# A prefix-sum diagonal kernel: small PSUM copies moved from ScalarE to VectorE, and the last tiles cut up differently

## The chip, the cores and the metric

The kernel runs on one core of a Trainium2 chip. The metric is the device time of one execution in microseconds (us). Executions of one kernel agree within about 0.3%, and all runs told of here are of the fast state with the full granted TensorE clock (1.0). Engines are named as in the profile: PE (matrix multiply), DVE (VectorE), ACT (ScalarE), POOL (GpSimd), SP (the engine that issues the input DMAs).

## The reference

```python
def reference(x):                      # x: (4, 4224, 4224) float32
    ps = np.cumsum(np.cumsum(x, axis=1), axis=2)
    diag = np.diagonal(ps, axis1=1, axis2=2)
    return np.cumsum(diag, axis=1).astype(np.float32)   # (4, 4224)
```

All of x, 285 MB, has to be read once. The output is 68 KB.

## The kernel before

Each batch is cut into 33 tiles of 128 rows and all 4224 columns (2112 KB). For tile I the kernel makes three things: ACT sums each row up to the end of the diagonal block (`rp_full`); DVE multiplies the diagonal block with a triangular mask (`du`, with its row sums in `rp_du`) and adds the tile into a running column sum `acc`; PE sums `du` and a block of `acc` over the rows into `cp_ps`. From these comes one number per row, `s = rp_full - rp_du + cp_ps`. Two prefix passes on PE then turn the numbers of one batch into its output. Each pass needs small results copied from PSUM to SBUF between its matmuls:

```python
def cumsum_pass1(x_sb):
    nc.tensor.matmul(cs_ps, lhsT=u_incl, rhs=x_sb, start=True, stop=False)
    nc.tensor.matmul(a_ps, lhsT=x_sb, rhs=ones_col, start=True, stop=True)
    nc.scalar.copy(a_sb, a_ps)                     # ACT
    nc.tensor.matmul(p_ps, lhsT=a_sb, rhs=u_strict[0:NB, 0:NB], ...)
    nc.scalar.copy(p_sb, p_ps)                     # ACT
    nc.tensor.matmul(cs_ps, lhsT=ones_row, rhs=p_sb, start=False, stop=True)
    nc.vector.tensor_copy(t_sb, cs_ps)             # DVE
# pass 2: again two ACT copies (a2_sb, p2_sb); its result stays in PSUM (ot_ps)
```

In the last batch the passes run early, over tiles 0 to 30, and the last two tiles are added by short extra matmuls. The last tile (32) comes in ten pieces, 1408, 896, 640, 384, 256 and five times 128 columns, so that its sums can start before all of it is there:

```python
for ci, (c0, c1) in enumerate(last_chunks):        # ten pieces
    nc.scalar.activation(out=act_scratch[:, c0:c1], in_=xt[:, c0:c1],
                         func=Copy, accum_out=rp_parts[:, ci : ci + 1])
    # ... pre += rp_parts of this piece (DVE), but for the last piece
# ... after the loop, in this order:
pre2 = pre - rp_du[:, LAST]; pre2 += cp_ps[:, LAST]        # DVE
delta = pre2 + rp_parts[:, NPART - 1]                      # DVE
nc.tensor.matmul(ot_ps[LAST], lhsT=delta, rhs=ramp_ut, start=False, stop=True, ...)
nc.scalar.copy(ot_sb[LAST], ot_ps[LAST])
nc.scalar.dma_start(out=out_by_block[b, LAST], in_=ot_sb[LAST])   # rows 0 to 31 went out before
```

Of the kernel before, what the change touches and what calls it, by code (L numbers as in the profile page):

```python
# [9 lines left out]
FP32 = mybir.dt.float32  # L10
# [4 lines left out]
def kernel(  # L15
# [5 lines left out]
    nc = tc.nc  # L21

    B, H, W = x.shape
# [8 lines left out]
    fast_tail = (LAST % 32 == 0) and NB >= 4 and B >= 1  # L32
# [43 lines left out]
    def make_last_chunks():  # L76
        sizes = []
        remaining = W
        first = True
        while remaining > 0:  # L80
            if first:
                size = min(remaining, max(P, (remaining // (3 * P)) * P))
                first = False
            else:
                size = max(P, min((2 * sizes[-1] + P) // (3 * P) * P, remaining))
            size = min(size, remaining)
            sizes.append(size)
            remaining -= size
        chunks = [(W - sizes[0], W)]
        start = 0  # L90
        for s in sizes[1:]:
            chunks.append((start, start + s))
            start += s
        assert start == W - sizes[0]
        return chunks

    last_chunks = make_last_chunks() if fast_tail else [(0, W)]
    NPART = len(last_chunks)

    def cumsum_pass1(x_sb):  # L100
# [4 lines left out]
        a_sb = smalls.tile([NB, 1], FP32, name="a_sb")  # L105
        nc.scalar.copy(a_sb, a_ps)  # L106
# [4 lines left out]
        p_sb = smalls.tile([1, NB], FP32, name="p_sb")  # L111
        nc.scalar.copy(p_sb, p_ps)  # L112
        nc.tensor.matmul(cs_ps, lhsT=ones_row, rhs=p_sb, start=False, stop=True)  # L113
        t_sb = smalls.tile([P, NB], FP32, name="t_sb")
        nc.vector.tensor_copy(t_sb, cs_ps)  # L115
        return t_sb

    def cumsum_pass2_transposed(t_sb, ot_ps):
# [3 lines left out]
        a2_sb = smalls.tile([NB, 1], FP32, name="a2_sb")  # L122
        nc.scalar.copy(a2_sb, a2_ps)  # L123
# [4 lines left out]
        p2_sb = smalls.tile([1, NB], FP32, name="p2_sb")  # L128
        nc.scalar.copy(p2_sb, p2_ps)  # L129
# [4 lines left out]
    for b in range(B):  # L134
# [4 lines left out]
        rp_parts = perbatch.tile([P, NPART + 1], FP32, name="rp_parts")  # L139
# [7 lines left out]
        if last_batch:  # L147
            s31mat = smalls.tile([P, 32], FP32, name="s31mat")
            nc.vector.memset(s31mat, 0.0)
            pre = smalls.tile([P, 1], FP32, name="pre")  # L150
            delta = smalls.tile([P, 1], FP32, name="delta")
            s31 = smalls.tile([P, 1], FP32, name="s31")

        for I in range(NB):
# [16 lines left out]

            chunked = last_batch and I == LAST and NPART > 1
            xt = tiles.tile([P, W], FP32, name="xt")
            if not chunked:
# [8 lines left out]
            if not chunked:  # L183
                nc.scalar.activation(  # L184
                    out=act_scratch[:, 0 : P * (I + 1)],
                    in_=xt[:, 0 : P * (I + 1)],
                    func=mybir.ActivationFunctionType.Copy,
                    accum_out=rp_full[:, I : I + 1],
                )
            else:  # L190
                for ci, (c0, c1) in enumerate(last_chunks):
# [13 lines left out]
                    elif 1 < ci < NPART - 1:  # L205
# [5 lines left out]
                        )  # L211

# [43 lines left out]
        if not last_batch:  # L256
# [8 lines left out]
            nc.scalar.copy(ot_sb, ot_ps)  # L265
# [3 lines left out]
        nc.vector.tensor_tensor(  # L269
            out=s31,  # L270
            in0=rp_full[:, LAST - 1 : LAST],
            in1=rp_du[:, LAST - 1 : LAST],
            op=mybir.AluOpType.subtract,
        )
        nc.vector.tensor_tensor(
            out=s31,
            in0=s31,
            in1=cp_ps[:, LAST - 1 : LAST],
            op=mybir.AluOpType.add,
        )  # L280
        nc.vector.tensor_copy(out=s31mat[:, 31:32], in_=s31)
        nc.tensor.matmul(
            ot_ps[0:32, :],
            lhsT=s31mat,
            rhs=ramp_ut,
            start=False,
            stop=True,
            skip_group_check=True,
        )
        nc.tensor.matmul(  # L290
            ot_ps[LAST : LAST + 1, :],
            lhsT=s31,
            rhs=ramp_full,
            start=False,
            stop=False,
            skip_group_check=True,
        )
        nc.scalar.copy(ot_sb[0:LAST, :], ot_ps[0:LAST, :])
        nc.gpsimd.dma_start(out=out_by_block[b, 0:LAST, :], in_=ot_sb[0:LAST, :])

        if NPART == 1:
            base_ap = rp_full[:, LAST : LAST + 1]
        elif NPART == 2:
            base_ap = rp_parts[:, 0:1]
        else:
            base_ap = pre
        pre2 = smalls.tile([P, 1], FP32, name="pre2")
        nc.vector.tensor_tensor(
            out=pre2,
            in0=base_ap,  # L310
            in1=rp_du[:, LAST : LAST + 1],
            op=mybir.AluOpType.subtract,
        )
        nc.vector.tensor_tensor(
            out=pre2,
            in0=pre2,
            in1=cp_ps[:, LAST : LAST + 1],
            op=mybir.AluOpType.add,
        )
        if NPART > 1:  # L320
            nc.vector.tensor_tensor(
                out=delta,
                in0=pre2,
                in1=rp_parts[:, NPART - 1 : NPART],
                op=mybir.AluOpType.add,
            )
        else:
            delta = pre2
# [43 lines left out]
```

## Time and profile before

| | before |
|---|---|
| time, median of 13 runs | 686.09 us |
| span of the program in the profile | 684.0 us |
| last byte of x landed (semaphore updates in the trace) | 673.64 us |
| from there to the end of the span | 10.4 us |

From the page of the kernel before: busy time of the engines with their share of the span, then the busy share of DVE, ACT and the DMA engines in 40 slices, in tenths (9 is 90% or more), and the rate of the DMAs.

```profile
PE 146.1 (21%) x590; PEld 129.3 (19%) x590; DVE 326.4 (48%) x424; ACT 284.7 (42%) x304; POOL 4.0 (1%) x16
...
DVE  3876553321587654322078756432118775542211
ACT  1122344566312334556711234456661222454675
...
DMA  9999999999999999999999999999999999999991
GB/s 369 431 429 428 428 428 428 429 429 429 428 426 430 428 429 429 428 428 427 429 428 429 430 428 427 430 428 429 429 428 427 429 430 427 430 428 428 428 421 66
```

The DMA row is at 9 in every slice but the last. The rate is level at about 428 GB/s and no other engine is full. So in all but the last of the 40 slices the kernel moves at the speed of its input. The chain of waits (the chain of work that ended last, followed back; shares by engine and by line) says the same:

```profile
DMA 85%; DVE 6%; ACT 6%; issue 1%; PE 1%; SPq 0%; DVEq 0%; ACTq 0%
DMA xt<-in_x_dram 85%; ACT act_scratch L184 5%; DVE acc L249 5%; ACT act_scratch L192 1%; DVE du L214 0%; DVE acc L245 0%; PE cs_ps L113 0%; PE cs_ps L102 0%; SPq L175 0%; PE ot_ps L119 0%; PE ot_ps L329 0%; PE p_ps L108 0%; PE a_ps L104 0%; DVE t_sb L115 0%; ACT p_sb L112 0%
```

What is left for a change is the end. This is ACT's timeline there: start in us, duration in us, engine, source line, operation, out<-in with shapes, and in brackets how long ACT was idle before it and what ended the wait. (Each sum is followed by a 0.19 us step that reads its accumulator; those rows are left out, and the shorter pieces too.)

```profile
663.18 3.51 ACT L184 ACTIVATE act_scratch<-xt 128x3968 bf16<-128x3968 f32 x1 [1.54 <-DMA xt<-in_x_dram]
...
668.23 0.15 ACT L106 COPY a_sb<-a_ps 33x1 f32<-33x1 f32 x1 [1.45 <-PE a_ps L104]
668.74 0.18 ACT L112 COPY p_sb<-p_ps 1x33 f32<-1x33 f32 x1 [0.35 <-PE p_ps L108]
670.62 0.15 ACT L123 COPY a_sb<-a_ps 33x1 f32<-33x1 f32 x1 [1.71 <-PE a_ps L121]
671.13 0.18 ACT L129 COPY p_sb<-p_ps 1x33 f32<-1x33 f32 x1 [0.35 <-PE p_ps L125]
671.21 3.61 ACT L184 ACTIVATE act_scratch<-xt 128x4096 bf16<-128x4096 f32 x1
...
674.82 1.36 ACT L192 ACTIVATE act_scratch<-xt 128x1408 bf16<-128x1408 f32 x1
...
679.90 0.29 ACT L192 ACTIVATE act_scratch<-xt 128x128 bf16<-128x128 f32 x1
...
681.60 0.26 ACT L337 COPY ot_sb<-ot_ps 1x128 f32<-1x128 f32 x1 [1.17 <-PE ot_ps L329]
681.89 0.50 ACTq L338 DMA_DIRECT2D out_dram<-ot_sb  x1
```

Tile 31 had landed at 668.23, in the middle of this, but its sum (4096 columns, L184) starts at 671.21. Ahead of it in ACT's order stand four copies that each wait for PE. From then on ACT is never idle: tile 31, then ten pieces one after the other, until 680.28, the last accumulator read included. All pieces had landed by 673.64, so nothing here waits for data any more.

DVE's timeline at the very end shows what follows the last pieces: the additions into `pre`, two more for `rp_du` and `cp_ps`, and `delta` (L321), which PE waits for.

```profile
678.86 1.32 DVE L206 TENSOR_TENSOR pre<-pre,rp_parts 128x1 f32<-128x1 f32 x5 [0.24 <-ACT act_scratch L192]
680.22 0.16 DVE L308 TENSOR_TENSOR pre<-pre,rp_du 128x1 f32<-128x1 f32 x1
680.42 0.16 DVE L314 TENSOR_TENSOR pre<-pre,cp_ps 128x1 f32<-128x1 f32 x1
680.68 0.16 DVE L321 TENSOR_TENSOR delta<-pre,rp_parts 128x1 f32<-128x1 f32 x1
```

### The profile page before, as it was taken

To read this page: it belongs to the slowest core of one execution; us is meant where nothing else is said; L and a number is where in the kernel's file an instruction comes from. 1 tells how busy PE (TensorE), PEld (TensorE's weight loads), DVE (VectorE), ACT (ScalarE), POOL (GpSimd) and SP (SyncE) were. 2 spreads that over 40 slices of the span, in tenths; PEclk is the share of its full clock that TensorE was granted. 3 is DMA by queue.
4 is the path that set the end of the run, shared out by engine and by line. 5 is a ranking of instruction groups with operands and counts; after the bars stand their busy time and mean duration, and the time that the engine had idled before them with its cause. 6 is when DMAs were issued, how large, how long until landed. Compare 5 with 4: busy or idle time off the path is not lost.

```text
span 684.0 us, 2514 instructions
## 1 busy us (share of the span) xinstructions
PE 146.1 (21%) x590; PEld 129.3 (19%) x590; DVE 326.4 (48%) x424; ACT 284.7 (42%) x304; POOL 4.0 (1%) x16
## 2 busy tenths in 40 slices
PE   0121121221411212212132112121122221221213
PEld 0121121111311211112122112121122111111212
DVE  3876553321587654322078756432118775542211
ACT  1122344566312334556711234456661222454675
POOL 1000000000000000000000000000000000000000
DMA  9999999999999999999999999999999999999991
GB/s 369 431 429 428 428 428 428 429 429 429 428 426 430 428 429 429 428 428 427 429 428 429 430 428 427 430 428 429 429 428 427 429 430 427 430 428 428 428 421 66
DMA packets 20447, 285.69 MB, mean 418 GB/s; under 512 B 2336, under 2 KB 3282, under 8 KB 3666
## 3 DMA queue, kind: packets, MB, share of 16 engines
q1 hardware_dynamic: 20304, 285.48, 98.2%
q8 instruction: 4, 0.07, 0.0%
q0 software_dynamic: 128, 0.07, 0.0%
q14 instruction: 9, 0.07, 0.0%
q10 hardware_dynamic: 2, 0.00, 0.0%
HBM read 285.47 MB, written 0.07 MB: 417 GB/s over the span
## 4 chain that ended last, share of the span: by engine, by line
DMA 85%; DVE 6%; ACT 6%; issue 1%; PE 1%; SPq 0%; DVEq 0%; ACTq 0%
DMA xt<-in_x_dram 85%; ACT act_scratch L184 5%; DVE acc L249 5%; ACT act_scratch L192 1%; DVE du L214 0%; DVE acc L245 0%; PE cs_ps L113 0%; PE cs_ps L102 0%; SPq L175 0%; PE ot_ps L119 0%; PE ot_ps L329 0%; PE p_ps L108 0%; PE a_ps L104 0%; DVE t_sb L115 0%; ACT p_sb L112 0%
## 5 line engine op out<-in xcount | busy, mean ns | idle before, releaser
L184 ACT ACTIVATE act_scratch<-xt 128x128 bf16<-128x128 f32 (+10 forms) x131 | 262.5, 2004 | 378.4 <-DMA xt<-in_x_dram 378.4
L249 DVE TENSOR_TENSOR acc<-acc,xt 128x3968 f32<-128x3968 f32 (+30 forms) x124 | 283.6, 2287 | 0.0
L214 DVE CUSTOM_DVE_ANT_0 du<-xt,u_strict 128x128 f32<-128x128 f32 x132 | 38.5, 292 | 322.0 <-DMA xt<-in_x_dram 322.0
L224 PE MATMUL cp_ps<-ones_col,du 128*128 128x1 f32 x264 | 77.3, 362 | 512.0 <-DVE rp_du L214 512.0
L224 PEld LDWEIGHTS cp_ps<-ones_col,du 128*128 128x128 f32 x264 | 66.1, 311 | 524.3 <-DVE rp_du L214 513.7
L234 PE MATMUL cp_ps<-ones_col,acc 128*128 128x1 f32 x256 | 72.4, 352 | 0.0
L234 PEld LDWEIGHTS cp_ps<-ones_col,acc 128*128 128x128 f32 x256 | 70.0, 333 | 0.0
L184 ACT ACTIVATION_READ_ACCUMULATOR act_scratch<-xt 128x1 f32 x131 | 24.4, 186 | 0.0
L214 DVE DVE_READ_ACCUMULATOR2_ANT rp_du<- 128x1 f32 x132 | 10.9, 82 | 0.3
L245 DVE COPY acc<-xt 128x4096 f32<-128x4096 f32 x4 | 9.2, 2290 | 0.0
L257 DVE TENSOR_TENSOR s_sb<-rp_full,rp_du 128x33 f32<-128x33 f32 x3 | 0.6, 196 | 10.5 <-ACT act_scratch L184 10.5
L192 ACT ACTIVATE act_scratch<-xt 128x128 bf16<-128x128 f32 (+5 forms) x10 | 5.4, 537 | 0.0
L115 DVE COPY t_sb<-cs_ps 128x33 f32<-128x33 f32 x4 | 0.8, 194 | 9.0 <-PE cs_ps L113 9.0
L102 PE MATMUL cs_ps<-s_sb,u_incl 128*128 128x33 f32 x8 | 2.6, 413 | 11.7 <-DVE s_sb L260 8.9
L266 POOL DMA_DIRECT2D out_dram<-ot_sb x3 | 1.7, 575 | 511.8 <-ACT ot_sb L265 511.8
L102 PEld LDWEIGHTS cs_ps<-s_sb,u_incl 128*128 128x128 f32 x8 | 2.0, 312 | 12.0 <-DVE s_sb L260 9.2
L123 ACT COPY a_sb<-a_ps 33x1 f32<-33x1 f32 x4 | 0.6, 153 | 6.8 <-PE a_ps L121 6.8
L106 ACT COPY a_sb<-a_ps 33x1 f32<-33x1 f32 x4 | 0.6, 153 | 5.8 <-PE a_ps L104 5.8
L119 PE MATMUL ot_ps<-u_incl,t_sb 128*33 128x128 f32 x8 | 2.5, 422 | 1.1 <-DVE t_sb L115 1.1
L113 PE MATMUL cs_ps<-p_sb,u_incl 1*128 1x33 f32 x8 | 2.5, 408 | 1.1 <-ACT p_sb L112 1.1
L130 PE MATMUL ot_ps<-u_incl,p_sb 1*33 1x128 f32 x8 | 2.5, 416 | 1.1 <-ACT p_sb L129 1.1
L113 PEld LDWEIGHTS cs_ps<-p_sb,u_incl 1*128 1x128 f32 x8 | 2.0, 308 | 1.8 <-ACT p_sb L112 1.8
(50 smaller groups left out, 23.0 us busy)
## 6 DMA issues: line engine op xcount, KB each, us to landing
xt<-in_x_dram SPq DMA_DIRECT2D x131, 2112.0 KB, 27.2
xt<-in_x_dram SPq DMA_DIRECT2D x1, 704.0 KB, 23.8
xt<-in_x_dram SPq DMA_DIRECT2D x1, 448.0 KB, 24.4
xt<-in_x_dram SPq DMA_DIRECT2D x1, 320.0 KB
xt<-in_x_dram SPq DMA_DIRECT2D x5, 64.0 KB, 5.0
xt<-in_x_dram SPq DMA_DIRECT2D x1, 192.0 KB, 24.3
xt<-in_x_dram SPq DMA_DIRECT2D x1, 128.0 KB, 19.6
out_dram<-ot_sb POOLq DMA_DIRECT2D x3, 16.5 KB, 5.6
```

The lines of the kernel that those rows point to most:

```text
L102: nc.tensor.matmul(cs_ps, lhsT=u_incl, rhs=x_sb, start=True, stop=False)
L113: nc.tensor.matmul(cs_ps, lhsT=ones_row, rhs=p_sb, start=False, stop=True)
L119: nc.tensor.matmul(ot_ps, lhsT=t_sb, rhs=u_incl, start=True, stop=False)
L130: nc.tensor.matmul(ot_ps, lhsT=p2_sb, rhs=ones_row, start=False, stop=True)
L184: nc.scalar.activation(out=act_scratch[:, 0 : P * (I + 1)], in_=xt[:, 0 : P * (I + 1)], func=mybir.ActivationFunctionType.Copy, accum_out= ...
L192: nc.scalar.activation(out=act_scratch[:, c0:c1], in_=xt[:, c0:c1], func=mybir.ActivationFunctionType.Copy, accum_out=rp_parts[:, ci : ci ...
L214: nc.vector.tensor_tensor_reduce(out=du, in0=xt[:, P * I : P * (I + 1)], in1=u_strict, scale=1.0, scalar=0.0, op0=mybir.AluOpType.mult, op ...
L224: nc.tensor.matmul(cp_ps[:, I : I + 1], lhsT=du, rhs=ones_col, start=False, stop=False, skip_group_check=True,)
L234: nc.tensor.matmul(cp_ps[:, I : I + 1], lhsT=acc[:, P * I : P * (I + 1)], rhs=ones_col, start=False, stop=False, skip_group_check=True,)
L245: nc.vector.tensor_copy(out=acc[:, P * (I + 1) :], in_=xt[:, P * (I + 1) :])
L249: nc.vector.tensor_tensor(out=acc[:, P * (I + 1) :], in0=acc[:, P * (I + 1) :], in1=xt[:, P * (I + 1) :], op=mybir.AluOpType.add,)
L266: nc.gpsimd.dma_start(out=out_by_block[b], in_=ot_sb)
```

## The change

Its intent is to shorten this tail: take the copies out of ACT's order, fetch and sum tile 31 in halves, cut tile 32 into four pieces, give part of tile 30 to DVE, and send the output of the last batch in one DMA. Cut to its core:

```diff
+    last_chunks: four pieces, (2816,4224) (0,1280) (1280,2304) (2304,2816), not ten
+
+    def psum_to_sbuf(name, src):
+        dst = smalls.tile(list(src.shape), FP32, name=name)
+        nc.vector.tensor_copy(dst, src)
+        return dst
...
-        nc.scalar.copy(a_sb, a_ps)
+        a_sb = psum_to_sbuf("a_sb", a_ps)          # p_sb, a2_sb, p2_sb likewise, in all batches
...
+            split31 = last_batch and I == LAST - 1 and NPART > 1
+            if split31:
+                for (c0, c1) in ((0, W // 2), (W // 2, W)):
+                    nc.sync.dma_start(out=xt[:, c0:c1], in_=x[b, P*I : P*(I+1), c0:c1])
...
+            elif split31:        # two ACT sums, 0:2112 and 2112:4096, and a DVE addition
...
+            elif last_batch and I == LAST - 2 and NPART > 1:
+                half = P * (I + 1) - 1408          # ACT sums 0:2560, DVE the other 1408 columns
+                nc.vector.reduce_sum(out=rp_parts[:, NPART + 3 : NPART + 4],
+                                     in_=xt[:, half : P * (I + 1)], axis=X)
...
-            nc.scalar.copy(ot_sb, ot_ps)           # batches 0 to 2
+            nc.vector.tensor_copy(ot_sb, ot_ps)
...
-        nc.scalar.copy(ot_sb[0:LAST, :], ot_ps[0:LAST, :])
-        nc.gpsimd.dma_start(out=out_by_block[b, 0:LAST, :], in_=ot_sb[0:LAST, :])
+        with tc.high_priority():                   # around the whole tail
...
+            nc.scalar.copy(ot_sb, ot_ps)
+            nc.scalar.dma_start(out=out_by_block[b], in_=ot_sb)     # all 33 rows at once
```

More of the change, by code (lines that the diff above doesn't have):

```diff
@@ L30 @@
     N_TILE_BUFS = 6
-    fast_tail = (LAST % 32 == 0) and NB >= 4 and B >= 1
+    fast_tail = (LAST % 32 == 0) and NB >= 4
     consts = ctx.enter_context(tc.tile_pool(name="consts", bufs=1))
@@ L74 @@
     ones_row = u_incl[0:1, :]
-    def make_last_chunks():
-        sizes = []
-        remaining = W
-        first = True
-        while remaining > 0:
-            if first:
-                size = min(remaining, max(P, (remaining // (3 * P)) * P))
-                first = False
-            else:
-                size = max(P, min((2 * sizes[-1] + P) // (3 * P) * P, remaining))
-            size = min(size, remaining)
-            sizes.append(size)
-            remaining -= size
-        chunks = [(W - sizes[0], W)]
-        start = 0
-        for s in sizes[1:]:
-            chunks.append((start, start + s))
-            start += s
-        assert start == W - sizes[0]
-        return chunks
-    last_chunks = make_last_chunks() if fast_tail else [(0, W)]
+    if fast_tail and W >= 8 * P:
+        c_a = (W // 3) // P * P
+        c_d = min(4 * P, max(P, (W // 8) // P * P))
+        rem = W - c_a - c_d
+        c_b = max(P, (rem * 3 // 5) // P * P)
+        c_c = rem - c_b
+        sizes = [c_a, c_b, c_c, c_d]
+        assert all(s >= P for s in sizes) and sum(sizes) == W
+        last_chunks = [
+            (W - c_a, W),
+            (0, c_b),
+            (c_b, c_b + c_c),
+            (c_b + c_c, c_b + c_c + c_d),
+        ]
+    else:
+        last_chunks = [(0, W)]
     NPART = len(last_chunks)
+    def psum_to_sbuf(name, src):
+        dst = smalls.tile(list(src.shape), FP32, name=name)
+        nc.vector.tensor_copy(dst, src)
+        return dst
     def cumsum_pass1(x_sb):
@@ L104, in cumsum_pass1 @@
         nc.tensor.matmul(a_ps, lhsT=x_sb, rhs=ones_col, start=True, stop=True)
-        a_sb = smalls.tile([NB, 1], FP32, name="a_sb")
-        nc.scalar.copy(a_sb, a_ps)
+        a_sb = psum_to_sbuf("a_sb", a_ps)
         p_ps = psum_ph2.tile([1, NB], FP32, name="p_ps", tag="aux_ps")
@@ L110, in cumsum_pass1 @@
         )
-        p_sb = smalls.tile([1, NB], FP32, name="p_sb")
-        nc.scalar.copy(p_sb, p_ps)
+        p_sb = psum_to_sbuf("p_sb", p_ps)
         nc.tensor.matmul(cs_ps, lhsT=ones_row, rhs=p_sb, start=False, stop=True)
-        t_sb = smalls.tile([P, NB], FP32, name="t_sb")
-        nc.vector.tensor_copy(t_sb, cs_ps)
-        return t_sb
+        return psum_to_sbuf("t_sb", cs_ps)
     def cumsum_pass2_transposed(t_sb, ot_ps):
@@ L121, in cumsum_pass2_transposed @@
         nc.tensor.matmul(a2_ps, lhsT=t_sb, rhs=ones_col, start=True, stop=True)
-        a2_sb = smalls.tile([NB, 1], FP32, name="a2_sb")
-        nc.scalar.copy(a2_sb, a2_ps)
+        a2_sb = psum_to_sbuf("a2_sb", a2_ps)
         p2_ps = psum_ph2.tile([1, NB], FP32, name="p2_ps", tag="aux_ps")
@@ L127, in cumsum_pass2_transposed @@
         )
-        p2_sb = smalls.tile([1, NB], FP32, name="p2_sb")
-        nc.scalar.copy(p2_sb, p2_ps)
+        p2_sb = psum_to_sbuf("p2_sb", p2_ps)
         nc.tensor.matmul(ot_ps, lhsT=p2_sb, rhs=ones_row, start=False, stop=True)
@@ L138 @@
         rp_du = perbatch.tile([P, NB], FP32, name="rp_du")
-        rp_parts = perbatch.tile([P, NPART + 1], FP32, name="rp_parts")
+        rp_parts = perbatch.tile([P, NPART + 4], FP32, name="rp_parts")
         acc = perbatch.tile([P, W], FP32, name="acc")
@@ L150 @@
             pre = smalls.tile([P, 1], FP32, name="pre")
+            pre2 = smalls.tile([P, 1], FP32, name="pre2")
             delta = smalls.tile([P, 1], FP32, name="delta")
@@ L170 @@
                 cumsum_pass2_transposed(t_sb, ot_ps)
+            split31 = last_batch and I == LAST - 1 and NPART > 1
             chunked = last_batch and I == LAST and NPART > 1
             xt = tiles.tile([P, W], FP32, name="xt")
-            if not chunked:
+            if split31:
+                for (c0, c1) in ((0, W // 2), (W // 2, W)):
+                    nc.sync.dma_start(
+                        out=xt[:, c0:c1], in_=x[b, P * I : P * (I + 1), c0:c1]
+                    )
+            elif not chunked:
                 nc.sync.dma_start(out=xt, in_=x[b, P * I : P * (I + 1), :])
@@ L182 @@
             act_scratch = scratch.tile([P, W], BF16, name="act_scratch")
-            if not chunked:
-                nc.scalar.activation(
-                    out=act_scratch[:, 0 : P * (I + 1)],
-                    in_=xt[:, 0 : P * (I + 1)],
-                    func=mybir.ActivationFunctionType.Copy,
-                    accum_out=rp_full[:, I : I + 1],
-                )
-            else:
+            if chunked:
                 for ci, (c0, c1) in enumerate(last_chunks):
@@ L211 @@
                         )
+            elif split31:
+                half = W // 2
+                nc.scalar.activation(
+                    out=act_scratch[:, 0:half],
+                    in_=xt[:, 0:half],
+                    func=mybir.ActivationFunctionType.Copy,
+                    accum_out=rp_parts[:, NPART : NPART + 1],
+                )
+                nc.scalar.activation(
+                    out=act_scratch[:, half : P * (I + 1)],
+                    in_=xt[:, half : P * (I + 1)],
+                    func=mybir.ActivationFunctionType.Copy,
+                    accum_out=rp_parts[:, NPART + 1 : NPART + 2],
+                )
+                nc.vector.tensor_tensor(
+                    out=rp_full[:, I : I + 1],
+                    in0=rp_parts[:, NPART : NPART + 1],
+                    in1=rp_parts[:, NPART + 1 : NPART + 2],
+                    op=mybir.AluOpType.add,
+                )
+            elif last_batch and I == LAST - 2 and NPART > 1:
+                half = P * (I + 1) - 1408
+                nc.scalar.activation(
+                    out=act_scratch[:, 0:half],
+                    in_=xt[:, 0:half],
+                    func=mybir.ActivationFunctionType.Copy,
+                    accum_out=rp_parts[:, NPART + 2 : NPART + 3],
+                )
+                nc.vector.reduce_sum(
+                    out=rp_parts[:, NPART + 3 : NPART + 4],
+                    in_=xt[:, half : P * (I + 1)],
+                    axis=mybir.AxisListType.X,
+                )
+                nc.vector.tensor_tensor(
+                    out=rp_full[:, I : I + 1],
+                    in0=rp_parts[:, NPART + 2 : NPART + 3],
+                    in1=rp_parts[:, NPART + 3 : NPART + 4],
+                    op=mybir.AluOpType.add,
+                )
+            else:
+                nc.scalar.activation(
+                    out=act_scratch[:, 0 : P * (I + 1)],
+                    in_=xt[:, 0 : P * (I + 1)],
+                    func=mybir.ActivationFunctionType.Copy,
+                    accum_out=rp_full[:, I : I + 1],
+                )
             du = dupool.tile([P, P], FP32, name="du")
@@ L264 @@
             cumsum_pass2_transposed(t_sb, ot_ps)
-            nc.scalar.copy(ot_sb, ot_ps)
+            nc.vector.tensor_copy(ot_sb, ot_ps)
             nc.gpsimd.dma_start(out=out_by_block[b], in_=ot_sb)
             continue
-        nc.vector.tensor_tensor(
-            out=s31,
-            in0=rp_full[:, LAST - 1 : LAST],
-            in1=rp_du[:, LAST - 1 : LAST],
-            op=mybir.AluOpType.subtract,
-        )
-        nc.vector.tensor_tensor(
-            out=s31,
-            in0=s31,
-            in1=cp_ps[:, LAST - 1 : LAST],
-            op=mybir.AluOpType.add,
-        )
@@ L281 @@
-        nc.vector.tensor_copy(out=s31mat[:, 31:32], in_=s31)
-        nc.tensor.matmul(
-            ot_ps[0:32, :],
-            lhsT=s31mat,
-            rhs=ramp_ut,
-            start=False,
-            stop=True,
-            skip_group_check=True,
-        )
-        nc.tensor.matmul(
-            ot_ps[LAST : LAST + 1, :],
-            lhsT=s31,
-            rhs=ramp_full,
-            start=False,
-            stop=False,
-            skip_group_check=True,
-        )
-        nc.scalar.copy(ot_sb[0:LAST, :], ot_ps[0:LAST, :])
@@ L299 @@
-        nc.gpsimd.dma_start(out=out_by_block[b, 0:LAST, :], in_=ot_sb[0:LAST, :])
-        if NPART == 1:
-            base_ap = rp_full[:, LAST : LAST + 1]
-        elif NPART == 2:
-            base_ap = rp_parts[:, 0:1]
-        else:
-            base_ap = pre
-        pre2 = smalls.tile([P, 1], FP32, name="pre2")
-        nc.vector.tensor_tensor(
-            out=pre2,
-            in0=base_ap,
-            in1=rp_du[:, LAST : LAST + 1],
-            op=mybir.AluOpType.subtract,
-        )
@@ L314 @@
-        nc.vector.tensor_tensor(
-            out=pre2,
-            in0=pre2,
-            in1=cp_ps[:, LAST : LAST + 1],
-            op=mybir.AluOpType.add,
-        )
-        if NPART > 1:
-            nc.vector.tensor_tensor(
-                out=delta,
-                in0=pre2,
-                in1=rp_parts[:, NPART - 1 : NPART],
+        with tc.high_priority():
+            nc.vector.tensor_tensor(
+                out=s31,
+                in0=rp_full[:, LAST - 1 : LAST],
+                in1=rp_du[:, LAST - 1 : LAST],
+                op=mybir.AluOpType.subtract,
+            )
+            nc.vector.tensor_tensor(
+                out=s31,
+                in0=s31,
+                in1=cp_ps[:, LAST - 1 : LAST],
@@ L325 @@
                 op=mybir.AluOpType.add,
             )
-        else:
-            delta = pre2
-        nc.tensor.matmul(
-            ot_ps[LAST : LAST + 1, :],
-            lhsT=delta,
-            rhs=ramp_ut,
-            start=False,
-            stop=True,
-            skip_group_check=True,
-        )
-        nc.scalar.copy(ot_sb[LAST : LAST + 1, :], ot_ps[LAST : LAST + 1, :])
-        nc.scalar.dma_start(
-            out=out_by_block[b, LAST : LAST + 1, :],
-            in_=ot_sb[LAST : LAST + 1, :],
-        )
+            nc.vector.tensor_copy(out=s31mat[:, 31:32], in_=s31)
@@ new lines @@
+            nc.tensor.matmul(
+                ot_ps[0:32, :],
+                lhsT=s31mat,
+                rhs=ramp_ut,
+                start=False,
+                stop=True,
+                skip_group_check=True,
+            )
+            nc.tensor.matmul(
+                ot_ps[LAST : LAST + 1, :],
+                lhsT=s31,
+                rhs=ramp_full,
+                start=False,
+                stop=False,
+                skip_group_check=True,
+            )
+            if NPART == 1:
+                base_ap = rp_full[:, LAST : LAST + 1]
+            elif NPART == 2:
+                base_ap = rp_parts[:, 0:1]
+            else:
+                base_ap = pre
@@ new lines @@
+            nc.vector.tensor_tensor(
+                out=pre2,
+                in0=base_ap,
+                in1=rp_du[:, LAST : LAST + 1],
+                op=mybir.AluOpType.subtract,
+            )
+            nc.vector.tensor_tensor(
+                out=pre2,
+                in0=pre2,
+                in1=cp_ps[:, LAST : LAST + 1],
+                op=mybir.AluOpType.add,
+            )
+            if NPART > 1:
+                nc.vector.tensor_tensor(
+                    out=delta,
+                    in0=pre2,
+                    in1=rp_parts[:, NPART - 1 : NPART],
+                    op=mybir.AluOpType.add,
+                )
+            else:
+                delta = pre2
@@ L345 @@
+            nc.tensor.matmul(
+                ot_ps[LAST : LAST + 1, :],
+                lhsT=delta,
+                rhs=ramp_ut,
+                start=False,
+                stop=True,
+                skip_group_check=True,
+            )
+            nc.scalar.copy(ot_sb, ot_ps)
+            nc.scalar.dma_start(out=out_by_block[b], in_=ot_sb)
 _INS = ['x']
```

## The prediction

> **What bounds the kernel now.** The input stream does. The page's slices show DMA at 9 tenths in every slice but the last, about 428 GB/s, and the chain of waits is 85% input DMA. At 5.05 us for each 2112 KB tile no other engine is full (DVE 48%, ACT 42%). The last piece of the last tile lands at 673.64 us (semaphore updates in the trace); the span ends at 684.0, the measured time is 2.2 us more. So only the 10.4 us after the stream are open to this change.
>
> **What the tail does now (timeline of ACT and DVE).** Tile 31 of the last batch landed at 668.23, but ACT starts its row sum only at 671.21: ACT runs in order and first makes four small copies for the prefix passes, the last at 671.13. Then it is never idle: 3.61 us for tile 31, then ten pieces of tile 32 from 674.82 to 680.29 (starts 0.29 us apart for 128 columns, 1.36 for 1408). All had landed by 673.64, so ACT, not DMA, ends the chain. Then `delta` on DVE (680.68), matmul (0.6), ACT copy, output DMA at 681.89, end 684.0.
>
> **What the change does there.**
> 1. The four copies go to DVE; ACT no longer waits for the passes: about 3.0 us.
> 2. Tile 31 arrives and is summed in halves: the first half, landing near 665.7, is summed (1.95 us) before the second lands at 668.2. ACT is done with tile 31 near 670.1, not 674.8.
> 3. Tile 32 in four pieces (1408, 1280, 1024, 512) instead of ten: 1.36+1.25+1.04+0.61 = 4.3 us of ACT instead of 5.4. Landings reckoned from 5.05 us a tile: 669.95, 671.5, 672.7, 673.3. ACT then runs nearly without a gap and ends near 674.6.
> 4. Tile 30: 1408 columns move to a DVE reduction. The Trainium skill, "VectorE: DVE Perf Modes", perf-mode tier table, gives tensor_reduce 1x only: I estimate 1.5 to 1.6 us; no run shows it yet. ACT waits for data there anyway, so pass 1 moves forward by tenths: off the path.
> 5. One output DMA of 33 rows after everything, instead of 32 early and one late: maybe 0.3 us longer at the end.
> 6. In batches 0 to 2 DVE may stall up to 4 us at a batch border. About five tiles (25 us) are in flight, so the stream shouldn't notice: 0.
>
> The ScalarE model, 186 ns + 0.833 ns per element, neighbours overlapping by 93 ns (Trainium skill, "ScalarE: Activation LUTs", What ACT_TABLE_LOAD costs), agrees with the trace (3.61 us for 4096 columns).
>
> **Sum.** `delta` starts near 674.7 instead of 680.68: -6.0 us, +0.3 for the output DMA. Predicted 680.5 us (0.8% less), range 679.5 to 682.0. The stream's end plus the closing steps put over 2% out of reach. Chances: faster by over 2% 0.5%, within 2% 98.5%, slower 1%.
>
> **What would show each step right or wrong.** ACT's first half of tile 31 starts near 665.7, the second near 668.3, no ACT copy between (1, 2). The last ACT piece ends at 674.4 to 675 (3). The DVE reduction takes 1.5 to 1.6 us and the stream stays near 428 GB/s in all slices (4, 6). From the start of `delta` to the end of the span: now 3.3 us, then 3.3 to 3.8 (5).
>
> **What would make it wrong.** DVE, also in order, now holds the passes: if the scheduler places a copy that waits for PE ahead of an addition that `delta` needs, up to 2 us come back. The 33-row output may land later than supposed. Splitting tile 31 could make the stream end later.

## The result

The kernel after takes 680.31 us (median of 8 runs, 680.16 to 680.60) against 686.09 us (13 runs). The ratio is 0.9916, with a 95% interval of 0.9907 to 0.9926. Ratios here are the mean time of one kernel's fast runs over that of the other's fast runs of the same rounds, so they are not quite the ratio of the medians. Below, "slower" and "less" without a reference mean differences of such medians. The small ones between kernels of different calls rest on the kernel before having stayed at 686.09 to 686.22 us in all calls.

One more thing has to be known before small differences are read. The measured time is longer than the program's span in the profiler, and every timed run has both. The excess is nearly constant within one kernel but not the same for all: 2.0 to 2.1 us for the kernels before and after and for `split31_only`, `last_on_act`, `no_split31`, `lean` and `quiet` below, but 1.7 us for `copies_only`, `pieces_only`, `border_on_act`, `after_ten`, `dubufs33` and `combo` (1.8 to 2.0 for `no_dve30`). What makes these 0.35 us isn't known; they lie outside the program's span. The main result isn't touched: the median span goes from 684.1 us to 678.2, 5.9 less. Where a kernel of the 1.7 us kind is compared with one of the other kind, the median span is given beside the time.

The page of the kernel after, its DMA slices and rates, and then its chain of waits:

```profile
DMA  9999999999999999999999999999999999999994
GB/s 366 429 429 429 429 429 429 425 428 427 427 430 430 429 428 427 427 428 429 427 429 429 428 429 427 427 427 429 428 429 429 429 426 428 426 428 429 428 424 203
```

```profile
DMA 82%; DVE 9%; ACT 6%; PE 1%; issue 1%; SPq 0%; DVEq 0%; ACTq 0%
DMA xt<-in_x_dram 82%; DVE acc L288 7%; ACT act_scratch L245 5%; DVE acc L284 1%; DVE du L253 1%; ACT act_scratch L185 0%; PE cs_ps L110 0%; ACT act_scratch L213 0%; PE ot_ps L114 0%; PE cs_ps L101 0%; SPq L175 0%; DVE p_sb L96 0%; DVE a_sb L96 0%; PE p_ps L106 0%; PE p_ps L119 0%
```

The stream is what it was: 9 in all slices but the last, the same rate. The last slice, however, moved 203 GB/s instead of 66, since less empty time stands behind the last bytes. ACT's timeline at the end, accumulator reads left out again:

```profile
663.41 2.34 ACT L227 ACTIVATE act_scratch<-xt 128x2560 bf16<-128x2560 f32 x1 [1.58 <-DMA xt<-in_x_dram]
...
665.96 1.96 ACT L207 ACTIVATE act_scratch<-xt 128x2112 bf16<-128x2112 f32 x1
...
668.49 1.86 ACT L213 ACTIVATE act_scratch<-xt 128x1984 bf16<-128x1984 f32 x1 [0.47 <-DMA xt<-in_x_dram]
...
670.34 1.36 ACT L185 ACTIVATE act_scratch<-xt 128x1408 bf16<-128x1408 f32 x1
...
671.70 1.27 ACT L185 ACTIVATE act_scratch<-xt 128x1280 bf16<-128x1280 f32 x1
...
672.97 1.04 ACT L185 ACTIVATE act_scratch<-xt 128x1024 bf16<-128x1024 f32 x1
...
674.01 0.61 ACT L185 ACTIVATE act_scratch<-xt 128x512 bf16<-128x512 f32 x1
...
675.62 0.26 ACT L374 COPY ot_sb<-ot_ps 33x128 f32<-33x128 f32 x1 [0.91 <-PE ot_ps L366]
675.91 0.59 ACTq L375 DMA_DIRECT2D out_dram<-ot_sb  x1
```

There are no copies between the sums any more. The second half of tile 31 starts at 668.49, just after it landed (668.46), and the four pieces follow without a gap until 674.72, the last accumulator read included. The last landing is at 673.57. The first three pieces landed at 670.18, 671.68 and 672.94 and are started 0.16, 0.02 and 0.03 us later (670.34, 671.70, 672.97): ACT now keeps pace with the landings, so from here on a further gain needs earlier landings. DVE's rows of the same stretch, from the reduction of tile 30 (L233) and two of the copies (L96) to the end:

```profile
663.35 1.62 DVE L233 TENSOR_REDUCE rp_parts<-xt 128x1 f32<-128x1408 f32 x1 [4.19 <-DMA xt<-in_x_dram]
...
667.48 0.15 DVE L96 COPY a_sb<-a_ps 33x1 f32<-33x1 f32 x1 [0.93 <-PE a_ps L103]
...
670.39 0.18 DVE L96 COPY p_sb<-p_ps 1x33 f32<-1x33 f32 x1 [0.36 <-PE p_ps L119]
...
674.14 0.16 DVE L199 TENSOR_TENSOR pre<-pre,rp_parts 128x1 f32<-128x1 f32 x1 [0.64 <-ACT act_scratch L185]
674.33 0.16 DVE L345 TENSOR_TENSOR pre<-pre,rp_du 128x1 f32<-128x1 f32 x1
674.53 0.15 DVE L351 TENSOR_TENSOR pre<-pre,cp_ps 128x1 f32<-128x1 f32 x1
...
674.79 0.16 DVE L358 TENSOR_TENSOR delta<-pre,rp_parts 128x1 f32<-128x1 f32 x1
```

`delta` (L358) starts at 674.79; it was 680.68. From there to the end of the span it takes 3.6 us; it was 3.3.

### The profile page after: what moved, and what is told of

Same layout as the page of the kernel before. It is cut to its first block, busy times and chain, and to the rows that moved or that the text cites. A ratio compares the mean times of both kernels' runs of the same rounds, so it can differ in the third digit from the quotient of the medians.

```text
span 678.4 us, 2481 instructions
## 1 busy us (share of the span) xinstructions
PE 146.0 (22%) x590; PEld 129.2 (19%) x590; DVE 329.8 (49%) x440; ACT 279.6 (41%) x274; POOL 3.5 (1%) x15
## 4 chain that ended last, share of the span: by engine, by line
DMA 82%; DVE 9%; ACT 6%; PE 1%; issue 1%; SPq 0%; DVEq 0%; ACTq 0%
DMA xt<-in_x_dram 82%; DVE acc L288 7%; ACT act_scratch L245 5%; DVE acc L284 1%; DVE du L253 1%; ACT act_scratch L185 0%; PE cs_ps L110 0%; ACT act_scratch L213 0%; PE ot_ps L114 0%; PE cs_ps L101 0%; SPq L175 0%; DVE p_sb L96 0%; DVE a_sb L96 0%; PE p_ps L106 0%; PE p_ps L119 0%
## 5 line engine op out<-in xcount | busy, mean ns | idle before, releaser
L245 ACT ACTIVATE act_scratch<-xt 128x128 bf16<-128x128 f32 (+10 forms) x129 | 255.4, 1980 | 392.4 <-DMA xt<-in_x_dram 392.4
L288 DVE TENSOR_TENSOR acc<-acc,xt 128x3968 f32<-128x3968 f32 (+30 forms) x124 | 283.5, 2286 | 0.0
L96 DVE COPY a_sb<-a_ps 33x1 f32<-33x1 f32 x8 | 1.2, 150 | 6.5 <-PE a_ps L103 3.4
L185 ACT ACTIVATE act_scratch<-xt 128x1408 bf16<-128x1408 f32 (+3 forms) x4 | 4.3, 1071 | 0.0
L233 DVE TENSOR_REDUCE rp_parts<-xt 128x1 f32<-128x1408 f32 x1 | 1.6, 1619 | 4.2 <-DMA xt<-in_x_dram 4.2
L227 ACT ACTIVATE act_scratch<-xt 128x2560 bf16<-128x2560 f32 x1 | 2.3, 2337 | 1.6 <-DMA xt<-in_x_dram 1.6
L96 DVE COPY p_sb<-p_ps 1x33 f32<-1x33 f32 x8 | 1.4, 181 | 2.3 <-PE p_ps L106 1.4
```

The costliest lines, as they stand in the source:

```text
L96: nc.vector.tensor_copy(dst, src)
L245: nc.scalar.activation(out=act_scratch[:, 0 : P * (I + 1)], in_=xt[:, 0 : P * (I + 1)], func=mybir.ActivationFunctionType.Copy, accum_out= ...
L288: nc.vector.tensor_tensor(out=acc[:, P * (I + 1) :], in0=acc[:, P * (I + 1) :], in1=xt[:, P * (I + 1) :], op=mybir.AluOpType.add,)
```

## The experiments

The theory is that after the stream ACT's order and ACT's load set the end. There were two rivals at the start. Rival A: fewer and larger transfers at the end let the stream itself end earlier. Rival B: the gain comes from the borders between batches. All kernels gave correct results, and all were timed in five rounds beside the kernel before.

### The copies alone

```diff
 # the kernel before, and only:
-        nc.scalar.copy(a_sb, a_ps)                 # and p_sb, a2_sb, p2_sb; ot_sb of batches 0 to 2
+        nc.vector.tensor_copy(a_sb, a_ps)
```

> The kernel before, with nothing changed but that the small PSUM copies of the prefix passes (and the output copy of batches 0 to 2) are made by DVE. Theory (ACT's order and its load after tile 31 set the end): ACT starts tile 31 at about 668.3 us instead of 671.2, the ten pieces still follow without a gap, so about 2.9 us less, 683.2. Rival A (the gain of the change comes from the input stream: fewer and larger transfers at the end): no gain, 686.1. Rival B (it comes from the batch borders in the stream): 2 us or more here too, but then the start of the last tile's DMA issue, and its landing, is earlier than 673.6.

Measured: 683.38 us, ratio 0.9959 (0.9947 to 0.9972), against 686.14. This is 2.8 us less, where the theory said 2.9. So close a hit is partly luck: the median span is only 2.4 us less (681.7 against 684.1). Tile 31 landed at 668.58 in this trace, 0.35 us later than in that of the kernel before, and starts at 668.66, as soon as it is there; `delta` starts 2.2 us earlier.

### The four pieces alone

```diff
 # the kernel before, and only:
-    last_chunks = make_last_chunks()
+    last_chunks = [(2816, 4224), (0, 1280), (1280, 2304), (2304, 2816)]
```

> The kernel before, with the last tile in the four pieces of the change instead of ten. Theory: ACT still starts tile 31 at 671.2; six fewer ACT pieces, 5.4 us to 4.3, so about 1.1 us less, 685.0. Rival A: the last landing moves from 673.6 to well earlier and most of the 5.9 us is gained. Rival B: no gain.

Measured: 684.34 us, ratio 0.9974 (0.9962 to 0.9987): 1.8 us less, more than expected. ACT needs 4.35 us from the start of the first piece to its end instead of 5.46, about as reckoned. What the expectation left out is the row of additions on DVE. With a last piece of 128 columns (0.29 us) three additions still stand between the last piece but one and `delta`, which starts 0.4 us after ACT's end. With a last piece of 512 columns (0.61 us) they run while ACT sums it, and `delta` starts 0.07 us after ACT's end. These two terms make 1.4 us; the median span is 1.5 us less (682.6 against 684.1), and the rest of the 1.8 lies outside the span. The last landing was 673.6 us, the same as before: rival A has no part in it.

### Tile 31 in halves alone

```diff
 # the kernel before, and only:
+            if split31:
+                # two DMAs, two ACT sums (0:2112, 2112:4096), one DVE addition
```

> The kernel before, with tile 31 fetched and summed in halves and nothing else. Theory: the wait for the copies is still in ACT's order ahead of both halves, so the halves only cost one more ACT start: 686.2 to 686.4, no gain. If the program's order lets the first half run before or between the copies, up to 2 us are gained, and ACT's timeline will show the first half before 671. Rival A: earlier end of the stream, a gain of 1 us or more with ACT still starting at 671.2.

Measured: 684.22 us, ratio 0.9971 (0.9958 to 0.9985): 1.9 us less, where no gain was the first guess. ACT's timeline shows the other case that the expectation named:

```profile
663.58 3.51 ACT L210 ACTIVATE act_scratch<-xt 128x3968 bf16<-128x3968 f32 x1 [1.58 <-DMA xt<-in_x_dram]
...
667.09 1.95 ACT L191 ACTIVATE act_scratch<-xt 128x2112 bf16<-128x2112 f32 x1
...
669.03 0.14 ACT L106 COPY a_sb<-a_ps 33x1 f32<-33x1 f32 x1
669.53 0.18 ACT L112 COPY p_sb<-p_ps 1x33 f32<-1x33 f32 x1 [0.35 <-PE p_ps L108]
669.61 1.85 ACT L197 ACTIVATE act_scratch<-xt 128x1984 bf16<-128x1984 f32 x1
...
671.46 0.13 ACT L123 COPY a_sb<-a_ps 33x1 f32<-33x1 f32 x1
```

The scheduler of the framework put the first half (L191) ahead of the copies and the second half between them. The half of tile 31 fills time in which ACT would have waited for PE. So moving the copies and halving the tile both attack the same wait, and their gains need not add. The totals don't show by how much they overlap: alone, the three parts give 2.8, 1.8 and 1.9 us, together 6.5, and the whole change 5.8; but in median spans they give 2.4, 1.5 and 1.9, together 5.8, and the whole 5.9 (in which the smaller parts below are contained).

### The copies of the last batch back on ACT

```diff
 # the kernel after, and only:
-        nc.vector.tensor_copy(dst, src)
+        (nc.scalar.copy if last_batch else nc.vector.tensor_copy)(dst, src)
```

> The kernel after, with the four pass copies of the last batch alone back on ACT; batches 0 to 2 keep them on DVE. Theory: ACT has to make the copies ahead of tile 31's halves, which then start near 670.6 to 671: 3.5 to 4 us of the gain are lost, 683.8 to 684.3. Rival B (batch borders): nothing is lost, 680.3. Rival A: nothing is lost.

Measured: 682.40 us, ratio 0.9945 (0.9932 to 0.9957): 2.1 us of the gain are lost, not 4. Again the first half of tile 31 runs before the copies (at 666.04). Only the second half waits behind them, until 670.42 instead of 668.5. Rival B, which expected no loss, is out for this part. The edit does a little more than its name says: the helper also makes the copy `t_sb`, which was DVE's in the kernel before, so this copy too is on ACT here (and, for batches 0 to 2, in `border_on_act`, `quiet` and `combo`).

### Tile 31 whole again

```diff
 # the kernel after, and only:
-            split31 = last_batch and I == LAST - 1 and NPART > 1
+            split31 = False
```

> The kernel after, but tile 31 comes as one transfer and one ACT pass. Theory: ACT starts it at 668.5 and ends at 672.1 instead of 670.3; the four pieces follow without a gap, delta at about 676.5 instead of 674.8: about 1.7 us slower than the kernel after, 682.0. Rival (the stream's end sets the end, ACT has slack): 680.3 to 680.6.

Measured: 682.00 us, ratio 0.9938 (0.9925 to 0.9950): 1.7 us slower than the kernel after, as the theory said.

### Tile 30 without the reduction on DVE

```diff
 # the kernel after, and only:
-            elif last_batch and I == LAST - 2 and NPART > 1:
+            elif False:
```

> The kernel after, but tile 30 is summed by ACT alone, no DVE reduction. The prediction called this reduction off the path, worth nothing: 680.3. Rival, from the trace of after: ACT ended tile 30 at 665.84 just before the first half of tile 31 landed at 665.88; with 1408 more columns it ends near 666.95, the half ends near 668.9 and the second half starts 0.4 us later than the 668.49 of now, so 0.4 us slower, 680.7.

Measured: 680.87 us, ratio 0.9921 (0.9909 to 0.9934), against 0.9916 (0.9907 to 0.9926) for the kernel after. The intervals overlap, so the times alone decide nothing. ACT's timeline is clear:

```profile
663.07 3.51 ACT L245 ACTIVATE act_scratch<-xt 128x3968 bf16<-128x3968 f32 x1 [1.57 <-DMA xt<-in_x_dram]
...
666.58 1.95 ACT L207 ACTIVATE act_scratch<-xt 128x2112 bf16<-128x2112 f32 x1
...
668.52 1.84 ACT L213 ACTIVATE act_scratch<-xt 128x1984 bf16<-128x1984 f32 x1
```

In this run the halves of tile 31 landed at 665.56 and 668.12. The first half starts 1.0 us after its landing, because tile 30 isn't done, and the second starts 0.4 us after its landing without any idle time before it. In the kernel after, the second half starts 0.03 us after its landing. The reduction is thus worth 0.4 us on the path by the timeline. (`delta` starts only 0.1 us later than in the trace of the kernel after, because tile 31 landed 0.3 us earlier in this one.) The prediction had called it off the path.

### The borders of batches 0 to 2 back on ACT

```diff
 # the kernel after, and only:
-        nc.vector.tensor_copy(dst, src)            # and ot_sb of batches 0 to 2
+        (nc.vector.tensor_copy if last_batch else nc.scalar.copy)(dst, src)
```

> The kernel after, but in batches 0 to 2 the copies are ACT's again; the last batch as after. Theory: the borders cost nothing in either form, 680.3 within 0.3. Rival B (the borders gave part of the gain): 681 or more.

Measured: 680.14 us, ratio 0.9911 (0.9898 to 0.9925), no loss (median span 678.4 against 678.2). The last landing is at 673.58, against 673.57 in the kernel after. Rival B is out altogether.

### Ten pieces again

```diff
 # the kernel after, and only:
+    last_chunks = make_last_chunks()               # ten pieces, as in the kernel before
```

> The kernel after, but the last tile in the ten pieces of the kernel before. Theory (ACT's load after the last landings, with the additions of DVE behind it): ACT needs 1.1 us more for ten pieces than for four, and the three additions no longer hide under the last piece (0.3 us): 1.4 us slower than the kernel after, 681.7. Rival A (the stream's end): a landing up to 1 us later and the rest unexplained.

Measured: 681.43 us, ratio 0.9931 (0.9918 to 0.9943): 1.1 us slower, where 1.4 were expected. Within the span it is 1.5 us (679.7 against 678.2), so the theory holds better than the times suggest. The last landing is 673.89 instead of 673.57 in these traces. That is no more than traces differ with the same ten pieces (673.64 in the kernel before, 674.02 in `copies_only`), so no effect of the size of the transfers is shown. Rival A is out as the main cause.

Two parts of the change were not tested alone: the single output DMA and the `tc.high_priority()` around the tail.

### Toward a faster version: half of PE's matmuls

While reading landings another limit came up. Each input DMA of 128 rows ends with 16 updates of its semaphore. The Trainium skill, "DMA: Bandwidth & Descriptors", section "Why a DMA increments its semaphore by 16 and not by 1", says that each of the DMA engines taking part adds one when its data has landed. The traces here have 16 updates per tile, too. So the time from the 15th to the 16th update is how far the last engine lies behind the others. This lag is 0.2 us for the first tile and 2.2 us for the last ones, so the last tile waits 2.2 us for one engine of sixteen. It grows in steps, and near the steps the queues that carry instructions move a packet (the profile doesn't say for which engine). The lines of these queues on the page of the kernel after (queue, kind: packets, MB, share):

```profile
q8 instruction: 4, 0.07, 0.0%
q14 instruction: 9, 0.07, 0.0%
```

The first reading blamed the packets of 16 KB (queue 8), because two of them (at 414 and 556 us) lay near two of the steps. PE has more instructions than any other engine, so PE's were halved:

```diff
 # the kernel after, and only:
+            if I >= 1:
+                nc.vector.tensor_tensor(out=du, in0=du, in1=acc[:, P*I : P*(I+1)], op=add)
             nc.tensor.matmul(cp_ps[:, I : I + 1], lhsT=du, rhs=ones_col, ...)
-            if I >= 1:
-                nc.tensor.matmul(cp_ps[:, I : I + 1], lhsT=acc[:, P*I : P*(I+1)], rhs=ones_col, ...)
```

> A try at a version that beats both, and a test of what delays the end of the stream. In both traces one of the 16 DMA engines ends each tile 2.2 us after the other fifteen from 557 us on; this lag grows by about 1 us just when the instruction queue moves a packet of 16 KB (at 414 and 556 us, 1.0 us each). Here DVE adds the accumulator's block into du, so PE has one matmul a tile instead of two, about half of its instructions. Theory: two 16 KB instruction packets instead of four, the lag at the end 1.0 to 1.4 us instead of 2.2, the whole tail 0.8 to 1.2 us earlier: 679.1 to 679.6. Rival (the lag is the engine's own, fetches have no part): the lag stays 2.2 us and the time 680.3. If the added DVE work (about 0.25 us a tile) slowed the stream, the time would be above 681.

Measured: 681.26 us, ratio 0.9929 (0.9916 to 0.9943): 1.0 us slower than the kernel after instead of 1 us faster. The same two lines of its page:

```profile
q14 instruction: 10, 0.08, 0.0%
...
q8 instruction: 2, 0.03, 0.0%
```

The 16 KB packets went from four to two as planned, yet the lag rose to 2.8 us. So the 16 KB packets were the wrong suspects. The expectation had also named time above 681 us as the sign that the added DVE work slows the stream. The traces speak against it: of the last piece the 15th update comes at 671.40 us in `lean` and at 671.39 in the kernel after; only the 16th is later (674.24 against 673.57), and that is 0.7 of the 1.0 us. Set beside the number of DVE instructions, the 8 KB packets tell more. This table is worked out from the traces (DVE instructions are all those of its sequencer, waits included; before the arrow the lag shortly before the packet, behind it shortly after):

```
kernel    8 KB packets at a lag step, us   DVE instructions run by then   all DVE instructions   lag of the last piece
before    83.4  246.0  402.7  565.2        63  193  319  449              567                    0.80 (pieces 1 to 8: 2.0 to 2.2)
after     83.7  241.1  392.8  550.2        63  193  319  450              573                    2.19
lean      73.2  182.1  326.9  454.0 576.1  67  182  321  450  575         696                    2.84

after:  392.8  0.2 -> 1.2      550.2  1.2 -> 2.2
lean:   326.9  0.3 -> 1.2      454.0  1.3 -> 2.3      576.1  1.9 -> 2.9
```

About every 128 DVE instructions 8 KB of them are fetched, and the lag of the last engine grows by about 1 us in the steps of the second list. At the first packets this measure grows less (0.6 us at 83.7 in the kernel after) or not at all (at 241.1), because there the 15th update falls behind as well. Added up over all 16 updates, each one's time after the first, the lateness grows by 1.1 and 1.0 us at these two packets.

The table shows only four of the nine 8 KB packets that the kernel after moves while it runs. The other five (114.1, 195.0, 331.7, 520.5 and 545.0 us) show no step in the lag of the last engine. Three of them come when ACT has run 64, 192 and 319 instructions and two when SP has run 81 and 209, so they are probably the fetches of these engines, again 128 instructions apart. At 195.0 and 331.7 the lateness added up grows by 0.5 and 0.6 us, and by 1.4 to 1.6 us at each 16 KB packet: these set other DMA engines back, and not the one that ends last. The kernel `lean` added 123 DVE instructions and with them a fifth packet.

### Toward a faster version: fewer DVE instructions

Of the 573 DVE instructions 130 are separate waits. `du` has three buffers, so before each tile DVE has to wait for PE as well as for the DMA. With 33 buffers, one for each tile of a batch, the wait at the border of a batch covers this, and nearly all of them fall away.

```diff
 # the kernel after, and only:
-    dupool = ctx.enter_context(tc.tile_pool(name="dupool", bufs=3))
+    dupool = ctx.enter_context(tc.tile_pool(name="dupool", bufs=33))
```

> The kernel after with 33 buffers for du instead of 3. In the traces so far the one DMA engine that ends last falls behind by 0.6 to 1.0 us each time that the DVE sequencer has run 64, 192, 320 and 448 instructions and the instruction queue moves a packet of 8 KB; the kernel after has 573 DVE instructions. With 33 buffers DVE needs no wait for PE before each du, and has about 459: the fourth fetch should come after about 670 us instead of at 550. Theory: the lag of tile 31 is 1.2 to 1.4 us instead of 2.2, and the time 679.3 to 680.0 (the late fetch may still hit the last piece). Rival (the packets are a coincidence): lag 2.2 and 680.3.

Measured: 679.15 us, ratio 0.9898 (0.9883 to 0.9913). DVE has 459 instructions. The packets at its steps come at 78.3, 276.2 and 478.4 us, and the fourth, which came at 550 before, at 672.1 (DVE counts 48, 175, 305 and 447; the first three come some 15 instructions earlier than expected). The lag of tile 31 is 1.2 us instead of 2.3, and tile 31 is complete at 667.37 instead of 668.46. The late packet hits the last piece: 1.5 us of lag, landing at 672.84. The time is 1.2 us less than that of the kernel after, and a buffer count was all that changed. Of the 1.2, the span shows 0.8 (medians 677.45 and 678.2), about what the last landing gained (672.84 instead of 673.57); the rest lies outside the span. The two intervals of the ratio touch (0.9913 and 0.9907), but the ranges of the runs lie far apart: 679.01 to 679.30 and 680.16 to 680.60.

```diff
 # as dubufs33, and the copies of batches 0 to 2 on ACT, as in border_on_act
```

> As the run before, and the copies of batches 0 to 2 on ACT, so DVE has about 440 instructions, fewer than 448: only three 8 KB packets at DVE counts 64, 192 and 320. Theory: lag at the end 1.2 to 1.4 us, last landing about 672.6 instead of 673.6, time 679.2 to 679.5. Rival: 680.2 with lag 2.2.

Measured: 679.53 us, ratio 0.9902 (0.9889 to 0.9916). DVE has 440 instructions and three packets at steps; the lag at the end is 1.0 us, the last landing 672.38. The theory of the fetches holds in the trace. That this kernel's runs (679.29 to 679.61) lie a little above those of `dubufs33` (679.01 to 679.30) was not expected. The two have the same median span, 677.45 us, so the difference lies wholly outside the span, and its cause stays open.

### A version that beats both

```diff
 # as quiet, and in the last batch:
+    last_chunks = [(2816, 4224), (0, 896), (896, 1792), (1792, 2432), (2432, 2816)]
+    # of the first piece ACT sums 896 columns, DVE 512 (part_a)
+    pre = part_a - rp_du[:, LAST] + cp_ps[:, LAST]          # DVE, before the last pieces
+    nc.vector.reduce_sum(out=four, in_=rp_parts[:, 0:4], axis=X)
-    nc.tensor.matmul(ot_ps[LAST], lhsT=delta, rhs=ramp_ut, stop=True, ...)
+    for part in (pre, four, rp_parts[:, 4:5]):              # PE adds them up in PSUM
+        nc.tensor.matmul(ot_ps[LAST], lhsT=part, rhs=ramp_ut, ...)
```

> A try at a version that beats both: the run before, and in the tail five pieces (1408, 896, 896, 640, 384), of whose first DVE sums 512 columns, and the last parts go straight to PE as matmuls that add up in PSUM, so that neither the row of additions nor delta stands behind the last piece. Reckoned: ACT ends 0.45 us earlier, one DVE step of 0.2 less, another matmul in line: 0.4 to 0.6 us less than the run before it, 678.7 to 679.0. If the lag theory fails, 679.7 to 680.0.

Measured: 678.91 us (678.83 to 679.05), ratio 0.9894 (0.9881 to 0.9908): 7.3 us less than the kernel before, against 5.8 for the kernel after. It is 0.6 us less than `quiet`, but only 0.25 us in the median span (677.2 against 677.45); its interval overlaps with those of `quiet` and `dubufs33`, so only the gain over the kernel after is taken as shown, and that by disjoint ranges of runs rather than by the intervals. ACT's and PE's timelines show why the new tail gives less than reckoned:

```profile
671.13 0.95 ACT L176 ACTIVATE act_scratch<-xt 128x896 bf16<-128x896 f32 x1
...
672.80 0.51 ACT L176 ACTIVATE act_scratch<-xt 128x384 bf16<-128x384 f32 x1
...
673.52 0.63 PE L355 MATMUL ot_ps<-ramp_ut,rp_parts 128*1 128x128 f32 x2
```

ACT's sum of the last piece ends at 673.31, against 673.43 in `quiet`: 0.12 us earlier and not 0.45. Its third piece landed only at 671.11, and ACT had to wait for it. The matmul of the last piece (L355) doesn't wait long behind the earlier ones: its weights are loaded from 673.45 on, 0.05 us after the read of the accumulator (673.40), and it starts 0.29 us before the last matmul of `quiet` (673.81). What the reckoning left out are the landings.

## Why the prediction was right

The predicted time was 680.5 us, the measured one is 680.31. Point by point:

- **What bounds the kernel.** Right. Slices and rate are the same after the change, and only the stretch behind the stream became shorter.
- **Step 1, the copies, 3.0 us.** Right in kind, a little large: alone 2.8 us by time and 2.4 by span. Put back in the last batch they cost 2.1 us.
- **Step 2, halves of tile 31.** Right. The halves start at 665.96 and 668.49 (predicted 665.7 and 668.3), and ACT is done with the tile at 670.34 (670.1). Undoing it costs 1.7 us.
- **Step 3, four pieces.** Right: 4.3 us of ACT, no gaps, end at 674.72 (674.6). Landings were 670.18, 671.68, 672.94 and 673.57 (669.95, 671.5, 672.7, 673.3), all about 0.2 us later, as is tile 30 in this trace. The prediction didn't list the three additions that now hide under the last piece, about 0.3 us; its start of `delta` (674.7, measured 674.79) had them in it.
- **Step 4, the DVE reduction.** Its duration is right: 1.62 us, estimated 1.5 to 1.6. That fits the 1x mode that the Trainium skill, "VectorE: DVE Perf Modes", perf-mode tier table, gives for it: DVE's addition of 1408 float32 columns, which that table has at 1x too, also takes 1.62 us in this trace (L288). "Off the path" was wrong. It frees ACT just when the first half of tile 31 lands and is worth 0.4 us by the timeline of the run without it. The prediction looked only at ACT's wait before tile 30 and not at the data that comes 2.6 us later, once tile 31 comes in halves. The total didn't suffer, because the sum took the first half to start at its landing, which without the reduction it could not have done. That was luck: two steps fitted together for a reason that the prediction had not seen.
- **Step 5, one output DMA, 0.3 us longer.** Right in these two traces: 3.6 us from `delta` to the end of the span instead of 3.3. No run isolates it, and with the same output DMA `no_split31` and `after_ten` show 3.4.
- **Step 6, the borders.** Right: 0 within the noise by the run that moves them back.

The prediction held because it followed ACT instruction by instruction against the landings. It did not add up separate gains, and so did not depend on whether they add.

## What to carry to other kernels

At the end of a kernel whose body runs at the speed of its input, write down when each piece lands and lay the order of the busy engine against it. A small copy that waits for another engine costs the whole wait when the next large piece of work stands behind it in the same order. Gains of changes that fill the same wait need not add, so reckon the end of the chain, not the sum of its parts. Look at the span beside the time before a difference of some tenths is explained: here 0.35 us came and went outside the span. When one DMA engine lags behind the others, look at the instruction fetches: here a buffer count that removed 114 waits from DVE was worth 0.8 us of the span (1.2 us of the time).

## What the Trainium skill lacked or had wrong

- "Runtime: NRT & Kernel Launch", section "Instruction fetch mechanics", says that an engine's instructions are refilled in blocks of 16 KiB (256 instructions), and that the cost is mostly hidden. In these traces those that go with DVE's counts come in packets of 8 KB, about one per 128 instructions of its sequencer (packets at DVE counts 63, 193, 319 and 450 in the kernel after).
- The same section has nothing of a cost to the data stream. With the input at full rate each such packet (0.33 us long) went with a step of 0.6 to 1 us, where one shows, in the lag of the last DMA engine, and it wasn't made up while the input ran at full rate: the lag at the end was 2.8 us with five packets, 2.2 with four, 1.0 with three. (In the kernel before, the lag fell from 2.1 to 0.8 us over the last two small pieces.) Which DMA engine it is, and why 0.33 us of packet cost it 1 us, the runs don't show.
- "ScalarE: Activation LUTs", section "What ACT_TABLE_LOAD costs", gives 186 ns + 0.833 ns per element, and the runs agree (a sum of 1408 columns lasts 1.36 us in the timelines). The step that reads the accumulator, 0.19 us after each sum in the timelines, of which about half overlaps with the next sum, has its cost on no page.
